# The opening of a hybrid decoder step: normalization in a written order, first weights by pairs of contraction tiles

## The chip, the core and the metric

The program runs on one core of a Trainium2 chip. A core has TensorE (PE, matmuls; PEld loads its stationary operand), VectorE (DVE), ScalarE (ACT), GpSimd (POOL) and SyncE (SP), each with an in-order queue of its own, and 16 DMA engines that move data between the chip's main memory and the on-chip memory SBUF. Matmuls write to PSUM, which has 8 banks of 128 x 512 fp32 here. The metric is the device time of one execution in microseconds (us); a change is judged by the medians of several executions.

## What is computed

One layer of a decoder with two branches, for 512 prompt rows behind 16 learned meta rows and for 8 x 4 sample rows with paged keys and values of the past (560 rows in all, model width 2048, 8 heads of 128):

```python
h = rmsnorm(x, g_pre)
q, k, v, ga, cb, cc, ch, gc, ma, mc = jnp.split(h @ w_in, split_offsets(), axis=-1)
a = attend(q, k, v, b_sb).reshape(bsz, t, D_ATTN) * jax.nn.silu(ga)      # stick-breaking attention
u = cc * ch
u_ext = jnp.concatenate([conv_hist, u], axis=1)
c = cb * causal_conv(u_ext, w_conv, b_conv) * jax.nn.silu(gc)
merged = sigmoid(ma + b_gate[:D_MODEL]) * (a @ w_pa) + sigmoid(mc + b_gate[D_MODEL:]) * (c @ w_pc)
y = x + rmsnorm(merged @ w_out, g_post)

def rmsnorm(x, g):
    y = x * lax.rsqrt(jnp.mean(x * x, axis=-1, keepdims=True) + RMS_EPS)
    return y * g
```

Products are wanted at fp32 accuracy. The kernel splits each operand into a high part in the format fp32r (a rounded copy, made by ACT) and a low part (the rest, made by DVE), and makes three products of them: high x high, low row part x high weight part, high row part x low weight part.

## The kernel before

The kernel is written in a layer that builds in-order queues for the engines from one program. A scheduler decides the order within each queue by a timing model of its own, except for instructions that are pinned (`pin`, which is `tc.keep_in_program_order`): these stay in the order in which the source gives them. `tc.high_priority` moves an instruction forward in the scheduler's choice.

The change lies in the opening stage, from the start to the end of the first four heads' query products ("the first weights", `FIRST = 4`):

- The 560 rows come as five tiles `xt` (tiles 0 to 3 of 128 rows, tile 4 of 48). For each, ACT squares and sums a row (`sq`, `ss`), takes a first inverse root by Ln and Exp (`rstd_of`), and five small operations refine it (`newton`, giving `rs`). DVE multiplies one half of the columns with `rs` and the broadcast gains `g_bc` (`hn`, 128x1024). PE transposes `hn` in 128x128 blocks into PSUM tiles of four blocks, ACT rounds each tile to `h_hi`, and DVE subtracts to get `h_lo`. Half 0 of a tile gives contraction tiles k = 0 to 7, half 1 gives k = 8 to 15.
- PSUM tiles of the transposes rotate over `z`, `z`, `z`, `tp` (`start_ps`). A tile is free again when DVE has made `h_lo` of it.
- The first weights come as eight raw tiles of 512 KB, two to a head (1024 rows of the weight by 128 columns each), with 512 bytes in a run. ACT makes `whi` of each. All four heads are first multiplied over 256 rows (tiles 0 and 1) with the high weight part alone, `q_part(..., (0, 1), ...)`. The low weight parts `wlo` are made later, from `low()`, after the other row tiles' normalization. Then each head gets its third product and the remaining 296 rows. The result of the 256 rows is copied to `qf` and stored.
- The queue SP issues the loads in the order x0, x1, two weight tiles, x4, six weight tiles, x2, x3.

After that the pool of the opening stage (`start`, called `sp` in the code) is closed, and what follows uses its room: `bsb` (head biases), `pt_i` (the page table of the sample rows' cache), `bg`, `wcv`, `stc`, and the tiles of the heads. The key, value and query products of the heads follow (`proj`, `gemm`, each of two 1024-row weight units with three split buffers, `whl`). Beside them run the steps of the sample rows' attention (`dec_step`): POOL reads page numbers out of `pt_i` into registers (32 of them), loads key pages `kpage` and queries `qb` (the latter from `q_scr`, to which POOL has stored the transposed queries `qn`), and DVE multiplies them (`pr`). `natural` transposes keys and values back into `nat`, one buffer, which POOL stores to the outputs.

Of the kernel before, what the change touches and what calls it, by code (L numbers as in the profile page):

```python
# [9 lines left out]
F32 = mybir.dt.float32  # L10
# [7 lines left out]
P = 128  # L18
D = 2048
# [41 lines left out]
def hybrid_step_kernel(  # L61
# [64 lines left out]
    def rstd_of(eng, out, ss, tmp, n, w=1, later=False):  # L126

        v, r, t = (tmp[:n, i * w:(i + 1) * w] for i in range(3))
        act.activation(r, ss, AF.Ln, bias=eps_c[:n], scale=1.0 / D)
        act.activation(r, r, AF.Exp, scale=-0.5)  # L130

        def newton(pin=lambda ins: ins):
            pin(eng.tensor_scalar(out=v, in0=ss, scalar1=1.0 / D, scalar2=EPS, op0=ALU.mult, op1=ALU.add))
# [3 lines left out]
            pin(eng.tensor_mul(out, r, t))  # L137
# [40 lines left out]
        g_ps.append(pt)  # L178

    def g_copy(c):  # L180
        pin(dve.tensor_copy(g_bc[:, c * 512:(c + 1) * 512], g_ps[c]))

    start_ps = cycle((z_ps, z_ps, z_ps, t_ps))

    def norm_stats(i):

        n = sum(r[0] for r in XT[i][0])
        xt = sp.tile([P, D], F32, name="xt", bufs=3)[:n]
        load_x(xt, i)
        ss = sp.tile([P, 1], F32, name="ss", bufs=5)[:n]  # L190
        sq = sp.tile([P, D], F32, name="sq", bufs=1)[:n]
        rs = sp.tile([P, 1], F32, name="rs", bufs=5)[:n]
        tmp = sp.tile([P, 4], F32, name="rtmp", bufs=5)
        with tc.high_priority():
            act.activation(sq, xt, AF.Square, accum_out=ss)
            newton = rstd_of(dve, rs, ss, tmp, n, later=True)
        return (i, n, xt, rs), newton

    def norm_half(c, x):


        i, n, xt, rs = x
        hn = sp.tile([P, D // 2], F32, name="hn", bufs=4)[:n]
        cs = slice(c * 1024, (c + 1) * 1024)
        pin(dve.scalar_tensor_tensor(out=hn, in0=xt[:, cs], scalar=rs, in1=g_bc[:n, cs],
                                     op0=ALU.mult, op1=ALU.mult))
        low = []
        for kq in range(2):
            pt = next(start_ps)()
            pv = pt[:, :4 * n].rearrange("p (k t) -> p k t", t=n)  # L210
            with tc.high_priority(2000):
                for k in range(4):
                    pe.transpose(out=pv[:, k, :], in_=hn[:, (4 * kq + k) * P:(4 * kq + k + 1) * P],
                                 identity=ident[:n, :n])
            k0 = 8 * c + 4 * kq
            for r0, r1, t0 in XT[i][1]:
                dst = (slice(None), slice(k0, k0 + 4), slice(t0, t0 + r1 - r0))
                with tc.high_priority(2000):
                    act.copy(h_hi[dst], pv[:, :, r0:r1])
                low.append((h_lo[dst], pv[:, :, r0:r1], h_hi.bitcast(F32)[dst]))  # L220

        def lows():
            for x in low:
                pin(dve.tensor_sub(*x))
        return lows


    def w_load(src, pl=wraw):
        raw = pl.tile([P, 8, P], F32, tag="raw", name="raw", bufs=5 if pl is wraw else 2 * FIRST - 5)
# [31 lines left out]
    def win_srcs(c):  # L261
        return [win[0:1024, c:c + P], win[1024:2048, c:c + P]]
# [20 lines left out]
    w_low = []

    def low(n=1):

        for _ in range(n):
            unit, raw = w_low.pop(0)
            lo = whl.tile([P, 8, P], F32R, tag="lo", name="wlo")
            pin(dve.tensor_sub(lo, raw, unit[0].bitcast(F32)))  # L290
            unit.append(lo)

    def q_part(o, ws, n, parts, start, stop):
        t0, t1 = START[n]
        for k in range(KD):
            for m in parts:
                pe.matmul(o, lhsT=ws[k // 8][m // 2][:, k % 8, :], rhs=(h_lo if m == 1 else h_hi)[:, k, t0:t1], start=(start and k + m == 0),
                          stop=(stop and k == KD - 1 and m == parts[-1]), skip_group_check=True)

    q_w, q_o = [], []  # L300

    def q_load(h):
        q_w.append([])
        for src in win_srcs(GATE_Q + h * P):
            n = len(w_low)
            raw = w_load(src, sp if n >= 5 else wraw)
            hi = sp.tile([P, 8, P], F32R, name="whi", bufs=2 * FIRST - 3) if n >= 3 else \
                whl.tile([P, 8, P], F32R, tag="hi", name="whi")
            act.copy(hi, raw)
            q_w[h].append([hi])  # L310
            w_low.append((q_w[h][-1], raw))

    x0, newton0 = norm_stats(0)
    x1, newton1 = norm_stats(1)
# [30 lines left out]
    l21 = norm_half(1, x2)
    l20()
    newton3(pin)
    l30 = norm_half(0, x3)
    l21()
    l31 = norm_half(1, x3)  # L350
    l30()
    low()
    l31()
    low()
    for h in range(FIRST):
        q_part(q_o[h], q_w[h], 0, (2,), False, True)
        qf = sp.tile([P, 256], F32, name="qf", bufs=2)
        act.activation(qf, q_o[h], AF.Copy, scale=SCALE)
        pool.dma_start(qt_scr[h][:, 0:256], qf)
        q_o[h] = (z_ps if h < 3 else mm_ps)()[:, :START[1][1] - START[1][0]]  # L360
        q_part(q_o[h], q_w[h], 1, (0, 1, 2), True, True)
        low(min(len(w_low), 2))
    stx.close()


# [956 lines left out]
```

## Time and profile before

| | |
|---|---|
| three runs, us | 1642.79, 1644.03, 1644.74 (median 1644.03) |
| profiled execution, us | 1641.85; its span from first to last instruction 1640.3 |
| mean granted TensorE clock of that execution | 0.99 |
| PE busy | 1594.9 us of the span, 97% |
| DVE, ACT, POOL busy | 1251.8, 970.1, 232.4 us |
| PE busy in 0 to 27, 27 to 54, 54 to 86.5 us | 15.08, 24.27, 32.50 us |
| last first-weights product starts | 86.27 us |

Busy times are what an engine worked, not what it had to; a PE that is busy need not be at its peak, since matmuls overlap. A row of the timeline gives the start, the length, the engine, the source line, the operation, out<-in with shape and count, and in brackets the idle time of that engine just before with the instruction that ended it. The stage tables give the busy time of each engine in a stretch, with PEclk, the clock that the throttle granted (1.00 is full).

### The profile page before, as it was taken

The page shows a single profiled execution, that of the slowest core. Times are in us where ns is not written, and L with a number is a line of the kernel's source. Part 1 is how long each engine was busy: PE and PEld are TensorE (multiplying, and loading weights), DVE is VectorE, ACT ScalarE, POOL GpSimd, SP SyncE. Part 2 cuts the span into 40 slices and gives each one's busy share as a digit, 9 for nine tenths or more (in the row PEclk, how much of TensorE's full clock was granted, in tenths as well). Part 3 has the DMA queues.
Part 4 walks back from the last instruction along what each step waited for, and adds up shares of the span by engine and source line. Part 5 has one row for each costly group of instructions (what it writes and reads, how often), then busy time and mean ns, then how long its engine had stood idle before and what let it go on. Part 6 is the DMA issues. An engine that isn't in the chain of part 4 may idle for free.

```text
span 1640.3 us, 31584 instructions
## 1 busy us (share of the span) xinstructions
PE 1594.9 (97%) x12176; PEld 1531.3 (93%) x12176; DVE 1251.8 (76%) x1707; ACT 970.1 (59%) x2529; POOL 232.4 (14%) x414
## 2 busy tenths in 40 slices
PE   7999999999999999999999999999999999999996
PEld 6999999999999999999999999989867699999995
DVE  4537887797988988888988888876555567877774
ACT  5237887745765655655677667685544543455552
POOL 0033233322101010101011010013122110000000
PEclk7999999999999999999999999999999999999998
DMA  9255454445544444443455454446887555433336
GB/s 228 70 179 152 155 160 139 146 128 170 157 147 136 136 135 122 127 142 111 137 164 161 149 174 148 135 125 204 283 261 222 172 152 179 154 106 94 104 87 216
DMA packets 306492, 252.72 MB, mean 154 GB/s; under 512 B 11457, under 2 KB 276741, under 8 KB 305237
## 3 DMA queue, kind: packets, MB, share of 16 engines
q1 hardware_dynamic: 277605, 159.73, 34.1%
q0 software_dynamic: 28016, 88.80, 16.5%
q8 instruction: 95, 1.56, 0.4%
q10 hardware_dynamic: 720, 2.17, 0.4%
q14 instruction: 56, 0.46, 0.1%
HBM read 217.95 MB, written 32.71 MB: 153 GB/s over the span
## 4 chain that ended last, share of the span: by engine, by line
PE 75%; ACT 6%; DMA 5%; DVE 5%; issue 3%; POOL 0%; DVEq 0%; SPq 0%; POOLq 0%; ACTq 0%
PE mm L887 24%; PE mm L252 24%; PE o L887 19%; ACT junk L695 3%; PE tp L784 2%; ACT whi L236 2%; DMA raw<-in_w_in 2%; PE z L614 1%; PE o L624 1%; DVE pr L689 1%; DVE wlo L237 1%; DMA gt<-gate_scr 1%; PE z L545 1%; PE z L887 1%; DMA kpage<-in_cache_k 1%
## 5 line engine op out<-in xcount | busy, mean ns | idle before, releaser
L236 ACT CAST whi<-raw 128x1024 fp32r<-128x1024 f32 x251 | 263.1, 1050 | 258.5 <-PE o L887 79.3
L237 DVE TENSOR_TENSOR wlo<-raw,whi 128x1024 fp32r<-128x1024 f32 x251 | 306.4, 1221 | 58.0 <-ACT whi L236 46.1
L887 PE MATMUL mm<-h_hi,whi 128*128 128x272 f32 (+1 forms) x1152 | 333.5, 290 | 2.8 <-ACT whi L236 2.8
L887 PE MATMUL mm<-h_lo,whi 128*128 128x272 f32 (+1 forms) x1152 | 332.1, 288 | 0.0
L887 PE MATMUL mm<-h_hi,wlo 128*128 128x272 f32 (+1 forms) x1152 | 331.3, 290 | 0.0
L887 PE MATMUL o<-t_hi,whi 128*128 128x272 f32 (+1 forms) x864 | 252.2, 292 | 8.5 <-ACT o L901 5.9
L887 PE MATMUL o<-t_hi,wlo 128*128 128x272 f32 (+1 forms) x864 | 249.9, 289 | 1.4 <-DVE wlo L237 1.4
L887 PE MATMUL o<-t_lo,whi 128*128 128x272 f32 (+1 forms) x864 | 249.6, 289 | 0.0
L237 DVE TENSOR_TENSOR wlo<-s,whi 128x1024 fp32r<-128x1024 f32 x126 | 154.2, 1224 | 101.5 <-ACT whi L236 101.2
L887 PEld LDWEIGHTS mm<-h_hi,whi 128*128 128x128 f32 x1152 | 217.3, 189 | 5.5 <-ACT whi L236 3.7
L887 PEld LDWEIGHTS mm<-h_hi,wlo 128*128 128x128 f32 x1152 | 216.3, 189 | 0.6 <-DVE dr L412 0.4
L887 PEld LDWEIGHTS mm<-h_lo,whi 128*128 128x128 f32 x1152 | 216.8, 188 | 0.1
L695 ACT ACTIVATE junk<-pr 128x128 f32<-128x128 f32 x592 | 182.7, 309 | 28.3 <-DVE pr L689 16.1
L236 ACT CAST whi<-s 128x1024 fp32r<-128x1024 f32 x126 | 131.6, 1044 | 97.5 <-PE o L887 31.0
L252 PE MATMUL mm<-h_hi,whi 128*128 128x280 f32 (+1 forms) x640 | 187.1, 293 | 0.0
L252 PE MATMUL mm<-h_hi,wlo 128*128 128x280 f32 (+1 forms) x640 | 187.0, 293 | 0.0
L252 PE MATMUL mm<-h_lo,whi 128*128 128x280 f32 (+1 forms) x640 | 186.7, 292 | 0.0
L887 PEld LDWEIGHTS o<-t_hi,whi 128*128 128x128 f32 x864 | 162.7, 188 | 15.1 <-ACT o L901 7.0
L887 PEld LDWEIGHTS o<-t_hi,wlo 128*128 128x128 f32 x864 | 162.9, 189 | 2.3 <-DVE wlo L237 2.2
L887 PEld LDWEIGHTS o<-t_lo,whi 128*128 128x128 f32 x864 | 163.4, 189 | 0.0
L689 DVE TENSOR_TENSOR pr<-kpage,qb 128x1024 f32<-128x1024 f32 x128 | 152.3, 1218 | 8.4 <-DMA kpage<-in_cache_k 4.0
L252 PEld LDWEIGHTS mm<-h_hi,whi 128*128 128x128 f32 x640 | 120.5, 188 | 0.7
(389 smaller groups left out, 3398.2 us busy)
## 6 DMA issues: line engine op xcount, KB each, us to landing
raw<-in_w_in SPq DMA_DIRECT2D x192, 512.0 KB, 4.3
kpage<-in_cache_k POOLq DMA_DIRECT2D x64, 256.0 KB, 3.4
qb<-q_scr POOLq DMA_DIRECT2D x32, 512.0 KB, 5.3
vpage<-in_cache_v POOLq DMA_DIRECT2D x64, 256.0 KB, 5.7
raw<-in_w_out SPq DMA_DIRECT2D x32, 512.0 KB, 4.0
gate_scr<-g POOLq DMA_DIRECT2D x32, 272.0 KB, 3.2
gt<-gate_scr POOLq DMA_DIRECT2D x16, 544.0 KB, 4.2
raw<-in_w_pc SPq DMA_DIRECT2D x16, 512.0 KB, 5.8
```

Of the source, the lines that this page charges most:

```text
L236: act.copy(hi, x)
L237: dve.tensor_sub(lo, x, hi.bitcast(F32))
L252: pe.matmul(o, lhsT=w, rhs=r[:, t0:t1], start=(k == 0 and n == 0), stop=(k == nk - 1 and n == 2))
L545: pe.matmul(zt[:m, c0:c0 + n], lhsT=l[:, s0:s0 + m], rhs=r[:, ts:ts + n], start=(c0 == 0 and i == 0), stop=(i == 2), skip_group_check=True)
L614: pe.matmul(o, lhsT=l, rhs=x, start=False, stop=(i == len(ops) - 1), skip_group_check=True)
L624: pe.matmul(ot[:, ts - NMETA:ts - NMETA + n], lhsT=l[:m, st, :], rhs=x[:m, c0:c0 + n], start=False, stop=(g == GROUPS[-1] and i == 2), ski ...
L689: dve.tensor_mul(pr, kt.unsqueeze(1).broadcast_to([P, 2, 512]), qt))
L695: act.activation(junk, pr[:, t, h * P:(h + 1) * P], AF.Copy, accum_out=z_all[:, pg, b, 4 * hf + h, 2 * i + t:2 * i + t + 1])
L784: pe.matmul(po[32 * j:32 * (j + 1), :], lhsT=lhs, rhs=rhs, start=(pg == 0), stop=(pg == NPG), tile_position=(0, 32 * j), skip_group_check= ...
L887: pe.matmul(o, lhsT=l[:, k, :], rhs=r, start=(start and k == 0 and m == 0), stop=(stop and k == 7 and m == 2), skip_group_check=True)
```

## The change

- **Order.** All steps of the opening stage on PE, ACT, DVE and SP are pinned: `pin` stands on the loads of x, the squares, Ln and Exp, the transposes, the `h_hi` copies, and the products. The source gives one order for all.
- **Gains.** Of the four copies that make `g_bc`, DVE keeps two and ACT makes two.
- **First weights by contraction tiles.** `q_load` now loads two contraction tiles k (256 weight rows) for all four heads at once: 512 KB in runs of 2 KB. `q_chunk(c)` makes, for k = 2c and 2c + 1, all three products of each head over the 256 rows. Both weight parts of all eight raw tiles stay in SBUF until the remaining 296 rows are multiplied.
- **PSUM.** Two heads share one bank (two tiles `mm` instead of three `mm` and one `o`); the freed `o` joins the rotation of the transposes.
- **Row tiles.** Tiles 0 and 1 come first, then chunks 0 to 7 of the products with tile 2 (between chunks 2 and 4) and tile 4 (before chunk 5) between them, and tile 3 after chunk 7. The refinement `newton` of tiles 2 and 4 is made on POOL.
- **Room.** The opening pool holds five `whi` and five `wlo` instead of five `whi` and three raw tiles. Tiles opened later, `bsb` and `pt_i` among them, now lie in its room.

```diff
     def load_x(xt, i):
...
-            nc.sync.dma_start(xt[r:r + n, :], {"p": xp, "m": meta_tokens, "s": xs}[src][r0:r0 + n, :])
+            tc.keep_in_program_order(
+                nc.sync.dma_start(xt[r:r + n, :], {"p": xp, "m": meta_tokens, "s": xs}[src][r0:r0 + n, :]))
...
     def g_copy(c):
-        pin(dve.tensor_copy(g_bc[:, c * 512:(c + 1) * 512], g_ps[c]))
-
-    start_ps = cycle((z_ps, z_ps, z_ps, t_ps))
+        copy = dve.tensor_copy if c < 2 else act.copy
+        pin(copy(g_bc[:, c * 512:(c + 1) * 512], g_ps[c]))
+
+    start_ps = cycle((z_ps, z_ps, z_ps, t_ps, o_ps))
...
-        with tc.high_priority():
-            act.activation(sq, xt, AF.Square, accum_out=ss)
-            newton = rstd_of(dve, rs, ss, tmp, n, later=True)
-        return (i, n, xt, rs), newton
+        pin(act.activation(sq, xt, AF.Square, accum_out=ss))
+        return (i, n, xt, rs), rstd_of(eng, rs, ss, tmp, n, later=True, fix=pin)
...
+    def q_load():
+        c = len(q_raw)
+        raw = wraw.tile([P, 8, P], F32, tag="raw", name="raw")
+        pin(nc.sync.dma_start(raw.rearrange("p (k h) c -> p k (h c)", k=2),
+                              win[2 * c * P:2 * (c + 1) * P, GATE_Q:GATE_Q + FIRST * P].rearrange(
+                                  "(k p) c -> p k c", p=P)))
+        q_raw.append(raw)
+
+    def q_part_tile(c, name):
+        if c < 3:
+            return whl.tile([P, 8, P], F32R, tag=name, name="w" + name)
+        return sp.tile([P, 8, P], F32R, name="w" + name, bufs=NC - 3)
...
+    def q_product(o, h, k, n, start, stop):
         t0, t1 = START[n]
...
+        hi, lo = (by_k(x[k // 2])[:, k % 2, h, :] for x in (q_hi, q_lo))
+        for m, (l, r) in enumerate(((hi, h_hi), (hi, h_lo), (lo, h_hi))):
+            pin(pe.matmul(o, lhsT=l, rhs=r[:, k, t0:t1], start=(start and m == 0), stop=(stop and m == 2),
+                          skip_group_check=True))
...
+    def q_chunk(c):
+
+        for h in range(FIRST):
+            for k in (2 * c, 2 * c + 1):
+                q_product(q_o[h], h, k, 0, k == 0 and h % 2 == 0, k == KD - 1)
...
+    newton1(pin)
+    q_high()
+    h10, l10 = norm_half(0, X[1])
+    h01()
     l00()
+    h11, l11 = norm_half(1, X[1])
+    h10()
+    X[4] = x_load(4)
...
+    l10()
+    q_high()
+    q_low()
+    h11()
+    q_chunk(0)
     l01()
+    q_low()
     l11()
...
+    q_chunk(7)
+    newton3(pin)
...
     for h in range(FIRST):
...
         q_o[h] = (z_ps if h < 3 else mm_ps)()[:, :START[1][1] - START[1][0]]
-        q_part(q_o[h], q_w[h], 1, (0, 1, 2), True, True)
-        low(min(len(w_low), 2))
+        for k in range(KD):
+            q_product(q_o[h], h, k, 1, k == 0, k == KD - 1)
     stx.close()
```

What the change makes of the queues is shown at three places. Line numbers of the changed kernel differ from those of the profile: L213 becomes L216, L297 becomes L321, L224 becomes L228, L205 becomes L209, L290 becomes L315, L373 and L374 become L436 and L437, L666 becomes L729.

PE, from the broadcast of the gains (L175) to the first products, before (the alternating rows of a tile's second half on `tp` are left out after the first two):

```order
L175 MATMUL z<-g_hl,pick 128x128 x8
L213 MATMUL z<-ident,hn 128x128 x9
L213 MATMUL tp<-ident,hn 128x128
...
L213 MATMUL z<-ident,hn 128x128 x8
L297 MATMUL mm<-h_hi,whi 128x256 x3
L213 MATMUL z<-ident,hn 128x128
L213 MATMUL tp<-ident,hn 128x128
...
L297 MATMUL mm<-h_lo,whi 128x256
L297 MATMUL mm<-h_hi,whi 128x256
```

The same place of PE in the changed kernel:

```order
L176 MATMUL z<-g_hl,pick 128x128 x8
L216 MATMUL z<-ident,hn 128x128 x12
L216 MATMUL tp<-ident,hn 128x128 x4
L216 MATMUL o<-ident,hn 128x128 x4
L216 MATMUL z<-ident,hn 128x128 x12
L321 MATMUL mm<-h_hi,whi 128x256
L321 MATMUL mm<-h_lo,whi 128x256
L321 MATMUL mm<-h_hi,wlo 128x256
```

All 32 transposes of tiles 0 and 1 now stand ahead of the first product, and each product with the low weight part stands beside the other two.

DVE, from the second refinement (its last row is L137) on, before:

```order
L137 TENSOR_TENSOR rs<-rtmp 128x1
L205 SCALAR_TENSOR_TENSOR hn<-xt,rs,g_bc 128x1024
L224 TENSOR_TENSOR h_lo<-z,h_hi 128x4x128 x3
L224 TENSOR_TENSOR h_lo<-tp,h_hi 128x4x128
L205 SCALAR_TENSOR_TENSOR hn<-xt,rs,g_bc 128x1024
L224 TENSOR_TENSOR h_lo<-z,h_hi 128x4x128 x3
L224 TENSOR_TENSOR h_lo<-tp,h_hi 128x4x128
```

DVE at the same place of the changed kernel:

```order
L138 TENSOR_TENSOR rs<-rtmp 128x1
L209 SCALAR_TENSOR_TENSOR hn<-xt,rs,g_bc 128x1024
L228 TENSOR_TENSOR h_lo<-z,h_hi 128x4x128 x2
L209 SCALAR_TENSOR_TENSOR hn<-xt,rs,g_bc 128x1024
L228 TENSOR_TENSOR h_lo<-o,h_hi 128x4x128
L228 TENSOR_TENSOR h_lo<-z,h_hi 128x4x128
L315 TENSOR_TENSOR wlo<-raw,whi 128x1024
L228 TENSOR_TENSOR h_lo<-z,h_hi 128x4x128
L228 TENSOR_TENSOR h_lo<-tp,h_hi 128x4x128
L315 TENSOR_TENSOR wlo<-raw,whi 128x1024
```

The second `hn` of tile 1 moved ahead of two of tile 0's four subtractions, and the low weight parts moved in among them.

POOL, from the identity matrix on (the 32 readings of `pt_i` follow each other before; `st_n` is the conv state, `bg_n` and `wc_n` are the gate biases and conv weights), before:

```order
masks.py:197 MEMSET ident 128x128
L373 DMA bsb<-in_b_sb 128x8
L374 DMA pt_i<-in_page_table 1x16x2
...
L149 AFFINE_SELECT tri<-tri 128x128
L666 TENSOR_LOAD pt_i
L666 ISA x2
...
L359 DMA qt_scr<-qf 128x256 x4
L377 DMA bg_n<-in_b_gate 32x128
```

POOL of the changed kernel, from the end of the refinement of tile 4 on (the rows that read `pt_i` go on, 32 in all, between the stores of the queries, `q_scr`):

```order
L138 TENSOR_TENSOR rs<-rtmp 48x1
L421 DMA qt_scr<-qf 128x256 x4
L436 DMA bsb<-in_b_sb 128x8
L437 DMA pt_i<-in_page_table 1x16x2
L440 DMA bg_n<-in_b_gate 32x128
...
L445 DMA st_n<-in_state_conv 16x1024
L535 DMA qt_scr<-qr 128x288 x2
L729 TENSOR_LOAD pt_i
L729 ISA x2
...
L541 DMA q_scr<-qn 32x128
```

The loads of `bsb` and `pt_i` moved from the start of the program to behind the stores of the first weights' results, where they wait for the last product of that stage, and the 32 readings moved with them.

More of the change, by code (lines that the diff above doesn't have):

```diff
@@ L122, in load_x, with rstd_of @@
         for n, src, r0 in XT[i][0]:
[L123 removed]
+            tc.keep_in_program_order(
+                nc.sync.dma_start(xt[r:r + n, :], {"p": xp, "m": meta_tokens, "s": xs}[src][r0:r0 + n, :]))
             r += n
[L126 removed]
+    def rstd_of(eng, out, ss, tmp, n, w=1, later=False, fix=lambda ins: ins):
         v, r, t = (tmp[:n, i * w:(i + 1) * w] for i in range(3))
[L129 to L130 removed]
+        fix(act.activation(r, ss, AF.Ln, bias=eps_c[:n], scale=1.0 / D))
+        fix(act.activation(r, r, AF.Exp, scale=-0.5))
         def newton(pin=lambda ins: ins):
@@ L189, in norm_stats @@
         load_x(xt, i)
+        return i, n, xt
+    def norm_stats(x, eng=dve):
+        i, n, xt = x
         ss = sp.tile([P, 1], F32, name="ss", bufs=5)[:n]
@@ L206, in norm_half @@
                                      op0=ALU.mult, op1=ALU.mult))
-        low = []
+        parts = []
         for kq in range(2):
@@ L210, in norm_half, with highs, w_load @@
             pv = pt[:, :4 * n].rearrange("p (k t) -> p k t", t=n)
[L211 to L214, printed above, removed]
+            for k in range(4):
+                pin(pe.transpose(out=pv[:, k, :], in_=hn[:, (4 * kq + k) * P:(4 * kq + k + 1) * P],
+                                 identity=ident[:n, :n]))
             k0 = 8 * c + 4 * kq
             for r0, r1, t0 in XT[i][1]:
[L217 to L220, printed above, removed]
+                parts.append(((slice(None), slice(k0, k0 + 4), slice(t0, t0 + r1 - r0)), pv[:, :, r0:r1]))
+        def highs():
+            for dst, src in parts:
+                pin(act.copy(h_hi[dst], src))
         def lows():
[L223 to L229, printed above, removed]
+            for dst, src in parts:
+                pin(dve.tensor_sub(h_lo[dst], src, h_hi.bitcast(F32)[dst]))
+        return highs, lows
+    def w_load(src):
+        raw = wraw.tile([P, 8, P], F32, tag="raw", name="raw")
         nc.sync.dma_start(raw, src.rearrange("(k p) c -> p k c", p=P))
@@ L282, in hybrid_step_kernel @@
     START = ((HM, HM + 256), (HM + 256, T))
[L283 to L293, printed above, removed]
-        t0, t1 = START[n]
[L295 to L314, printed above, removed]
@@ L318, in hybrid_step_kernel, with keep_warm @@
+    q_o = []
+    def q_chunk(c):
+        for h in range(FIRST):
+            for k in (2 * c, 2 * c + 1):
+                q_product(q_o[h], h, k, 0, k == 0 and h % 2 == 0, k == KD - 1)
+    def keep_warm(n):
+        pass
+    X = [None] * 5
+    X[0], X[1] = x_load(0), x_load(1)
+    for _ in range(3):
+        q_load()
+    X[2] = x_load(2)
+    X[0], newton0 = norm_stats(X[0])
     g_copy(0), g_copy(1)
+    g_copy(2), g_copy(3)
+    X[1], newton1 = norm_stats(X[1])
     newton0(pin)
-    l00 = norm_half(0, x0)
@@ L321, in hybrid_step_kernel @@
-    g_copy(2), g_copy(3)
-    l01 = norm_half(1, x0)
+    h00, l00 = norm_half(0, X[0])
+    keep_warm(4)
+    h01, l01 = norm_half(1, X[0])
+    keep_warm(6)
+    h00()
     newton1(pin)
-    l10 = norm_half(0, x1)
+    q_high()
+    h10, l10 = norm_half(0, X[1])
+    h01()
     l00()
+    h11, l11 = norm_half(1, X[1])
+    h10()
+    X[4] = x_load(4)
+    for _ in range(2):
+        q_load()
+    for i in range(2):
+        o = mm_ps()
+        q_o += [o[:, 0:256], o[:, 256:512]]
+    l10()
+    q_high()
@@ L345, in hybrid_step_kernel @@
[L345 to L356, printed above, removed]
+    q_high()
+    q_chunk(1)
+    X[2], newton2 = norm_stats(X[2], pool)
+    q_low()
+    for _ in range(2):
+        q_load()
+    q_chunk(2)
+    X[4], newton4 = norm_stats(X[4], pool)
+    newton2()
+    h20, l20 = norm_half(0, X[2])
+    q_high()
@@ new lines, in hybrid_step_kernel @@
+    q_low()
+    q_load()
+    X[3] = x_load(3)
+    h20()
+    q_chunk(3)
+    h21, l21 = norm_half(1, X[2])
+    q_high()
+    l20()
+    q_low()
+    h21()
+    newton4()
+    q_chunk(4)
+    h40, l40 = norm_half(0, X[4])
+    l21()
+    q_high()
+    h40()
+    q_low()
+    h41, l41 = norm_half(1, X[4])
+    q_chunk(5)
+    l40()
+    h41()
+    q_high()
+    q_low()
+    l41()
+    q_chunk(6)
+    q_high()
+    q_low()
+    X[3], newton3 = norm_stats(X[3])
+    q_chunk(7)
+    newton3(pin)
```

41 lines of the change are left out of this document (21 added, 20 removed).

## The prediction

> **What bounds the kernel now.** The page's first part says PE; so a gain has to be PE time that is idle or slow. The table by stage (columns: stretch and its length, PE, PEld, DVE, ACT and POOL busy, granted clock, share of the DMA engines, GB/s) shows where that is.
>
> ```profile
> PE 1594.9 (97%) x12176; PEld 1531.3 (93%) x12176; DVE 1251.8 (76%) x1707; ACT 970.1 (59%) x2529; POOL 232.4 (14%) x414
> 0.00:10.00 10.00, 8.62 (x42) 7.05 (x42) 4.00 (x17) 3.78 (x5) 2.15 (x9) 0.96 0.80 231
> 10.00:20.00 10.00, 3.88 (x16) 3.13 (x16) 5.13 (x10) 5.46 (x7) 0.00 (x0) 0.50 1.17 216
> 20.00:30.00 10.00, 5.58 (x26) 5.18 (x27) 5.06 (x7) 8.71 (x15) 0.00 (x0) 0.51 1.09 281
> 25.00:30.00 5.00, 3.62 (x18) 3.62 (x19) 2.93 (x4) 3.71 (x5) 0.00 (x0) 0.53 1.02 250
> 30.00:40.00 10.00, 10.00 (x89) 9.62 (x88) 5.46 (x10) 5.28 (x8) 0.00 (x0) 1.00 0.84 206
> 40.00:50.00 10.00, 7.52 (x65) 7.35 (x64) 7.71 (x24) 4.92 (x16) 0.00 (x0) 1.00 0.01 3
> 54.00:86.50 32.50, 32.50 (x247) 32.50 (x247) 12.43 (x12) 5.16 (x8) 2.21 (x4) 1.00 0.35 103
> 86.50:120.00 33.50, 33.50 (x264) 32.61 (x263) 10.93 (x16) 14.76 (x46) 11.98 (x22) 1.00 0.56 172
> ```
>
> From 10 to 30 us PE works 9.5 of 20 us, at half clock; 2.5 more are idle before 50; from 54 on it is full at full clock. The gain can only come from the first 54 us, and a loss can start anywhere that this full stretch is broken. PE's timeline says what it waits for in the weak part.
>
> ```profile
> 22.07 1.97 PE L213 MATMUL z<-ident,hn 128*128 128x128 f32 x8 [6.80 <-DVE h_lo L224]
> 26.39 1.01 PE L297 MATMUL mm<-h_hi,whi 128*128 128x256 f32 x3 [2.35 <-ACT h_hi L219]
> 29.33 0.41 PE L297 MATMUL mm<-h_lo,whi 128*128 128x256 f32 x1
> 29.54 0.36 PE L297 MATMUL mm<-h_hi,whi 128*128 128x256 f32 x1
> 30.09 0.28 PE L297 MATMUL mm<-h_hi,whi 128*128 128x256 f32 x1
> 30.21 0.28 PE L297 MATMUL mm<-h_lo,whi 128*128 128x256 f32 x1
> 44.93 1.06 PE L213 MATMUL z<-ident,hn 128*128 128x128 f32 x8 [2.48 <-DVE hn L205]
> 86.13 0.30 PE L297 MATMUL mm<-h_lo,whi 128*128 128x296 f32 x1
> 86.40 0.29 PE L252 MATMUL mm<-h_hi,whi 128*128 128x280 f32 x1
> ```
>
> It waits for the normalization chain (6.80 for an `h_lo`, 2.35 for an `h_hi`), not for weights. The first product starts at 26.39 and the opening ends at 86.40, where the first key product starts. The pitch of products is 0.21 in the slow clock (29.33 to 29.54) and 0.12 in the full one (30.09 to 30.21); with 296 columns it is 0.135 (86.13 to 86.40, two products); a transpose at full clock takes 0.11 ((1.06 - 0.27) / 7).
>
> **The front chain in the written order.** These rows of ACT and DVE give the durations.
>
> ```profile
> 10.28 1.91 ACT L195 ACTIVATE sq<-xt 128x2048 f32<-128x2048 f32 x1 [1.71 <-DMA xt<-in_x_prompt]
> 12.10 0.19 ACT L195 ACTIVATION_READ_ACCUMULATOR sq<-xt 128x1 f32 x1
> 12.19 1.03 ACT L309 CAST whi<-raw 128x1024 fp32r<-128x1024 f32 x1
> 13.12 0.29 ACT L129 ACTIVATE rtmp<-ss,eps_c 128x1 f32<-128x1 f32 x1
> 15.49 1.04 ACT L309 CAST whi<-raw 128x1024 fp32r<-128x1024 f32 x1 [2.08 <-DMA raw<-in_w_in]
> 16.44 0.20 ACT L130 ACTIVATE rtmp<-rtmp 128x1 f32<-128x1 f32 x1
> 22.82 0.57 ACT L219 CAST h_hi<-z 128x512 fp32r<-128x512 f32 x1
> 8.54 0.14 DVE L133 TENSOR_SCALAR rtmp<-ss 128x1 f32<-128x1 f32 x1
> 9.19 0.16 DVE L137 TENSOR_TENSOR rs<-rtmp 128x1 f32<-128x1 f32 x1
> 9.38 1.28 DVE L205 SCALAR_TENSOR_TENSOR hn<-xt,rs,g_bc 128x1024 f32<-128x1024 f32 x1
> 10.58 0.68 DVE L181 COPY g_bc<-mm 128x512 f32<-128x512 f32 x1
> 26.65 1.28 DVE L224 TENSOR_TENSOR h_lo<-z,h_hi 128x512 fp32r<-128x512 f32 x2
> L290 DVE TENSOR_TENSOR wlo<-raw,whi x8: 1209/1222/1227, 34.9 to 74.9; 128x1024 fp32r<-128x1024 f32 x8
> ```
>
> Before, the Exp of tile 1 stood behind two weight casts, the second of which waited for its raw tile, so it ran at 16.44 although its squares were done at 12.3. The written order puts nothing between. ACT gets two gain copies (about 0.57 each, the nearest row is the 128x512 `h_hi`), which push the squares of tile 1 from 10.28 to 10.6. Squares 1.91 + 0.19, Ln 0.29, Exp 0.20 end at 13.2; the five small operations, 0.81 from 8.54 to 9.35 in the rows, end `rs` at 14.1. DVE then, with starts 0.08 closer than the durations (9.38 to 10.58): `hn` 1.2, two `h_lo` 1.2, `hn` 1.2, two `h_lo` 1.2, one `wlo` 1.14, and one more `h_lo` 0.6, which frees the `z` that the last four transposes of tile 1 need: 20.7. Transposes at slow clock 0.84 and a hand-over of 0.15: **first product at 21.7 instead of 26.39.** The two copies DVE loses cost nothing there, since it waits for `rs` anyway.
>
> **From the first product to the end of the stage.** The count of products is the same: 192 of 256 rows x 0.12 = 23.0, 192 of 296 x 0.135 = 25.9, 48 transposes of tiles 2, 3, 4 x 0.11 = 5.3. The slow clock adds: in the rows PE's unbroken work began at 26.39 and the pitch changed at 29.7, 3.3 us later. If it takes 3.3 us again, 16 products cost 0.09 more each, 1.4; if the rise stays at 29.7 for another reason, 38 products, 3.4. I take 2.0, nearer to the first, since 26.39 is the only such start here. Waits in between I put at 0.6: one, for `hn` of tile 4's second half, as DVE makes the rest (`h_lo`, `wlo`) ahead of PE; the 296-row products start right behind tile 3, whose `h_lo` end within its transposes. Sum: 21.7 + 23.0 + 25.9 + 5.3 + 2.0 + 0.6 = **78.5 against 86.40, a gain of 7.9** (7.0 to 8.5 by the two ends of the clock and no wait).
>
> On the clock the Trainium skill has a rule, in "TensorE: Matmul & The Clock Gate", section "Part 1: The HAM clock gate": it rises after one fully busy window of about 3.4 us, and windows run free. The 3.3 us agree with it; by that rule the rise would fall between 25.1 and 28.5 here, and the stage would end between 77.9 and 79.4.
>
> Two heads in a bank, and both weight parts kept, cost room and no time: each `wlo` is made once, as before (8 x 1.22), earlier. The loads are hidden: the tables above give 2.3 MB by 10 us, 4.5 by 20, 7.3 by 30, and the order needs x0, x1 and three weight tiles (3.5 MB) by about 22 and x2, x4 and a fourth (5.4 MB) by 28.5. On SP, x4 waits for tile 0's buffer (its second `hn`, 12.0), and the fourth and fifth weight tiles behind it are needed 16 us later; the last three wait for buffers freed from about 20 on, and are needed from 37.
>
> **What lies behind the stage.** `bsb` and `pt_i` now wait on POOL for the stage's last product, and the 32 readings of `pt_i` move from hidden time to POOL's busiest stretch, ahead of the stores of the sample queries.
>
> ```profile
> L666 POOLq TENSOR_LOAD <-pt_i x32: 282/289/502, 9.6 to 28.3; - x32
> DMA to landing us min/median/max: 7.4/7.4/7.4
> bg_n<-in_b_gate POOLq DMA_DIRECT2D x1, 16.0 KB, 2.0
> 87.02 0.51 POOL L377 DMA_DIRECT2D bg_n<-in_b_gate  x1 [5.69 <-PE mm L297]
> 109.12 0.50 POOL L478 DMA_DIRECT2D q_scr<-qn  x1 [3.10 <-ACT qn L477]
> 117.48 5.70 DMA out<-nat
> 123.92 0.28 PE L445 MATMUL tp<-ident,raw 128*16 128x128 f32 x1 [1.13 <-ACT nat L443]
> ```
>
> A reading takes (28.3 - 9.6) / 31 = 0.60, all of them 19.3. `bg_n` was issued 0.6 behind the stage's end; two issues go ahead of it, and eight issues at about 0.53 put the first reading at +4.8 of the end, unless `pt_i` takes as long to land as at the start (7.4, then +8.5; the row of `bg_n`, issued in the same place, says 2.0). The fourth `q_scr` is issued at +24.1 if the DMA issues between the readings run beside them, +28.4 if after them (8 x 0.54), +32.1 if `pt_i` is late too; before it was +22.7 (109.12 - 86.40). So POOL's chain (query store, `qb`, then `out<-nat`, which frees `nat`) lags by 1.4 to 9.4; I take 4, near the case with `pt_i` quick. PE already waited 1.13 for `nat` at the value head's transposes, and these stand 27 products (3.4 us) later in PE's new order. So the wait becomes 1.13 + 4 - 3.4 = 1.7, **0.6 more than before** (bounds: 1.1 less, 6.0 more). From there on queues hold the same work.
>
> Total: 1641.85 (span 1640.3 and 1.55 around it) - 7.9 + 0.6 = 1634.5 for an execution like the profiled one. That one is 2.2 below the median, so against the median **1636.7**.
>
> **Refinement on POOL.** No row shows these small operations there. The nearest are POOL's selects of small tiles:
>
> ```profile
> L562 POOL TENSOR_SCALAR_AFFINE_SELECT r<-r x16: 190/308/3417, 144.0 to 292.1; 128x128 f32<-128x128 f32 x12, 16x16 f32<-16x16 f32 x4
> L562 POOL TENSOR_SCALAR_AFFINE_SELECT eA<-eA x4: 278/282/282, 161.9 to 303.7; 128x112 f32<-128x112 f32 x4
> ```
>
> Five at 0.28 are 1.4, five at the longest 17. Tile 2's Exp ends at about 26.0 by the durations above, and PE needs its first transposes only behind chunk 2 at 32.1, so up to some 4.8 us are covered. Beyond, DVE stands at `hn` with the `wlo` of later chunks queued behind it, and tile 4 comes behind tile 2 on POOL, so each us costs two. I take 1.5, by the medians.
>
> **Rivals.** (1) *The readings hold the queries.* At the far end, 9.4 of lag, PE loses 6.0 of the 7.9: 1644.03 - 7.9 + 6.0 = about 1642. For it: every issue on POOL stands in one queue, and nothing shows a reading beside an issue. Against: it needs the late `pt_i` as well. (2) *The other side: the refinement on POOL stretches.* At a length p the loss is 2 x (p - 4.8): the gain of 7.3 is gone at p = 8.5, the kernel is measurably slower above p = 10.1, and at p = 17 it takes about 1661. For it: the 3417 ns row, and DVE at work all the while beside it. Against: the medians. The Trainium skill, "SBUF — State Buffer", section "SBUF: two separate sides", calls the port pair of DVE and GpSimd an exclusive lock; whether the 3417 ns row is that, no run here shows. A form of this rival with a size of its own: if each of the five waits out one DVE instruction of 1.28, p is 5 x 1.56 = 7.8, and the time 1636.7 + 6.0 = 1642.7; that is what the lock of that page would make. (3) *A cast holds ACT.* In a strict order all of ACT stands behind a weight cast whose raw tile is late, as at 15.49 (2.08 of idle time). If the first raw tile comes one tile's transfer late (512 KB at 216 GB/s, 2.4 us) and the next one by 0.5, the first product starts at 24.6 and the time is about 1639.6. Against: x0, x1 and the first weight tiles lead the queue as before, and the first cast comes only at 14.1, where it ran at 12.19 without a wait.
>
> **How the numbers follow.** The forecast's case gets 60%: 1633 to 1639, from the ends of the clock, the waits and the smaller lags. Rival 1 gets 18%, rival 3 12%, rival 2 10%, half of it at 1642.7 and half slower than before. The range is 1633.0 to 1643.5: it takes in rivals 1 and 3 and leaves out the slow half of rival 2 and some of each end. 0.2% is 3.3 us, about what this kernel's runs can tell from no change. Faster by more (below 1640.7): nearly all of the forecast's case, most of rival 3 and a quarter of rival 1, 0.74. Within: most of rival 1, the mild rival 2, 0.18. Slower: 0.08.
>
> **What the new profile would show.** The first product at 21 to 22.5, PE full from there with a granted clock of 1.00 from about 26, no wait over 1 us, and the first key product at 78 to 80. The five operations of tile 2 on POOL within 2 us from about 26. On POOL, readings from about 5 us behind the stage's end, the last query store 24 to 32 behind it, and at the value head's transposes a PE wait of 0 to 4. I am wrong if PE waits for `hn` of tile 2 (rival 2), if ACT stands at a weight cast before 20 (rival 3), or if PE waits 5 us or more for `nat` (rival 1).

## The result: slower, though the opening stage is 10.6 us shorter

The changed kernel takes 1648.41 us in the median (1644.81 to 1651.14) against 1644.0; the ratio is 1.0029, with a 95% interval of 1.0021 to 1.0037. The execution that was profiled (1650.27) lies 1.9 above its median and that of the kernel before 2.2 below its own, so the two traces differ by 8.2 where the medians differ by 4.4.

The table by stage of the changed kernel, same columns as before:

```profile
10.00:20.00 10.00, 7.92 (x34) 6.78 (x35) 8.80 (x15) 8.64 (x15) 0.00 (x0) 0.50 1.05 216
20.00:30.00 10.00, 10.00 (x77) 10.00 (x77) 8.23 (x9) 7.20 (x11) 5.64 (x10) 0.87 1.00 307
100.00:110.00 10.00, 8.18 (x67) 7.91 (x65) 3.14 (x3) 3.97 (x8) 1.83 (x4) 1.00 0.41 117
110.00:120.00 10.00, 6.00 (x42) 5.79 (x41) 3.57 (x5) 2.58 (x13) 4.45 (x7) 0.91 0.77 246
390.00:400.00 10.00, 7.67 (x61) 7.45 (x60) 0.96 (x2) 3.78 (x4) 0.29 (x1) 1.00 0.93 283
400.00:410.00 10.00, 6.20 (x33) 6.20 (x34) 10.00 (x13) 4.84 (x19) 1.30 (x3) 0.66 0.29 85
```

The opening did what it was meant to: PE is full from 20 us on, but for 0.76 us at 38. What is new are two holes further back, at 100 to 120 us and at 390 to 410. Before, PE was full from 86.5 to 120, and between 390 and 410 it idled 2.2 us, in one wait (the last row is of the list of PE's waits: engine, output and line that waited, what it waited for; us, times, longest):

```profile
400.00:410.00 10.00, 7.76 (x62) 7.54 (x61) 6.04 (x7) 4.33 (x13) 1.58 (x3) 1.00 0.89 303
PE o L887 <- ACT o L901: 2.2, 1, 2.2
```

In PE's timeline of the changed kernel:

```profile
17.68 2.22 PE L216 MATMUL z<-ident,hn 128*128 128x128 f32 x8 [0.51 <-DVE hn L209]
19.55 0.56 PE L321 MATMUL mm<-h_hi,whi 128*128 128x256 f32 x1
22.77 0.28 PE L321 MATMUL mm<-h_hi,whi 128*128 128x256 f32 x1
22.89 0.28 PE L321 MATMUL mm<-h_lo,whi 128*128 128x256 f32 x1
38.45 0.42 PE L216 MATMUL o<-ident,hn 48*128 48x48 f32 x4 [0.76 <-DVE hn L209]
75.79 0.29 PE L256 MATMUL mm<-h_hi,whi 128*128 128x280 f32 x1
```

The first product starts at 19.55 (before 26.39), and the first key product at 75.79 (before 86.40). The two holes, in the list of PE's waits:

```profile
PE tp L505 <- DVE ks L511: 4.0, 1, 4.0
PE tp L538 <- ACT qn L540: 2.3, 2, 1.8
PE o L950 <- DVE c L976: 6.1, 1, 6.1
```

Both kernels issue the same matmuls, so the lead can be followed: take the start of PE's n-th matmul and subtract its start in the profile of the kernel before (a minus is earlier). Matmul 600 lies at 99 us of the kernel before, 1000 at 152, 2600 at 361, 3200 at 439, 12100 at 1615, near the end. The kernels below are those of the experiments, with one execution for each, so a row also holds what differs from execution to execution.

| kernel | 600 | 1000 | 2600 | 3200 | 12100 |
|---|---|---|---|---|---|
| changed | -10.6 | -4.0 | -3.9 | 5.3 | 8.2 |
| changed, second execution | -11.8 | -8.4 | -7.3 | 0.8 | 1.0 |
| pages early | -9.6 | -9.1 | -8.9 | -1.2 | 1.6 |
| copies first | -8.3 | -3.7 | -3.7 | 5.9 | 8.2 |
| query loads later | -11.8 | -7.8 | -6.7 | -2.5 | -0.3 |
| pages early and query loads later | -9.5 | -6.1 | -5.9 | -1.4 | -0.6 |
| pages and copies first, which gives the order of before at the switch | -11.1 | -9.7 | -9.7 | -8.3 | -9.6 |
| before, pages late | -0.7 | 3.7 | 3.8 | 5.2 | 8.8 |
| before, both loads late, which gives the order of the changed kernel at the switch | -3.3 | -0.7 | -0.7 | 7.5 | 10.1 |

**The first loss, 6.6 us between matmuls 600 and 1000 (3.4 in the second execution).** Rows of POOL, and one of ACT:

```profile
L729 POOLq TENSOR_LOAD <-pt_i x32: 283/288/499, 82.4 to 106.1; - x32
102.35 0.26 ACT L540 COPY qn<-tp 32x128 f32<-32x128 f32 x1 [4.15 <-DMA q_scr<-qn]
107.21 0.50 POOL L541 DMA_DIRECT2D q_scr<-qn  x1 [3.50 <-ACT raw L581]
110.39 2.18 POOL L744 DMA_DIRECT2D qb<-q_scr  x3 [2.68 <-issue]
```

The query loads of the kernel before:

```profile
111.41 2.18 POOL L681 DMA_DIRECT2D qb<-q_scr  x3 [1.78 <-issue]
```

The chain of waits of the changed kernel in that stretch:

```profile
110.39 5.54 DMA qb<-q_scr
116.03 1.23 DVE pr L752
117.25 0.19 DVE nat L510
117.44 0.21 DVE ks L511
```

The 32 readings run from 82.4 to 106.1, with the query stores among them. PE is held in two places. The first is `qn`, which has one buffer: ACT copies into it only when the store before has landed, and with the stores late ACT waits (4.15 in its row) and PE's transposes wait 2.3 us for ACT. In the kernel before POOL waited for `qn` (3.10 ahead of its store at 109.12) and not the other way round. The second is behind the queries. The query loads are issued 34.6 us behind the opening's end (110.39 - 75.79), where the kernel before needed 25.0 (111.41 - 86.40): a lag of 9.6. `pr` waits for the queries, DVE's two copies out of the key head's transposes stand behind `pr`, and the next transposes need the PSUM tile that these copies free (4.0 us). Behind that the granted clock falls (0.91 from 110 to 120).

**The second loss, 9.2 us between matmuls 2600 and 3200 (8.1 in the second execution).** This is where the gate products follow the heads; below it is called the switch. The rows are: of the chain of waits, the weight tile; of POOL, the loads of the sample rows' second part; of the answer on the tile `raw` between 387 and 390, the two issues and how long the tiles took to land (min/median/max).

```profile
387.84 11.93 DMA raw<-in_w_in
386.47 1.47 POOL L744 DMA_DIRECT2D qb<-q_scr  x2 [2.88 <-issue]
387.93 1.66 POOL L730 DMA_DIRECT2D kpage<-in_cache_k  x3
389.57 0.71 POOL L744 DMA_DIRECT2D qb<-q_scr  x1
L234 SPq DMA_DIRECT2D raw<-in_w_in x2: 367/368/368, 387.8 to 388.9; - x2
DMA to landing us min/median/max: 11.9/12.3/12.7
```

The same of the kernel before:

```profile
394.47 1.49 POOL L681 DMA_DIRECT2D qb<-q_scr  x2 [4.67 <-DMA raw<-in_w_in]
L230 SPq DMA_DIRECT2D raw<-in_w_in x2: 368/368/368, 388.7 to 389.8; - x2
DMA to landing us min/median/max: 4.1/4.1/4.1
```

In the changed kernel POOL's burst of 2.25 MB (three `qb` of 512 KB, three `kpage` of 256 KB) is issued from 1.4 us ahead of two weight tiles, which land after 12 us instead of 4. DVE idles (0.96 busy from 390 to 400), PE waits 6.1 us for `c`, and its clock falls (0.66 from 400 to 410). Before, the burst stood behind the landing of these tiles; a later tile, issued at 395.3 within it, took 9.8 us to land.

The burst is not all of this loss. Followed matmul by matmul, 3.0 us go between matmuls 2760 and 2800, around 380 us and so ahead of the burst, where PE waits 0.7, 0.6 and 0.7 in turn for `nat`, a weight cast and a `wlo`; 8.5 go between 2880 and 2920, at the wait for `c` and in the slow clock behind it; and 2.6 come back at the place where the kernel before has its own wait of 2.2.

### The profile page after: what moved, and what is told of

The parts are those of the page before. It is cut to its first block, busy times and chain, and to the rows that moved or that the text cites. A ratio compares the mean times of both kernels' runs of the same rounds, so it can differ in the third digit from the quotient of the medians.

```text
span 1648.7 us, 31575 instructions
## 1 busy us (share of the span) xinstructions
PE 1600.4 (97%) x12176; PEld 1536.7 (93%) x12176; DVE 1246.8 (76%) x1695; ACT 970.9 (59%) x2531; POOL 236.4 (14%) x424
## 4 chain that ended last, share of the span: by engine, by line
PE 74%; ACT 6%; DMA 6%; DVE 4%; issue 3%; DVEq 0%; POOL 0%; SPq 0%; ACTq 0%; POOLq 0%
PE mm L950 24%; PE mm L256 24%; PE o L950 19%; ACT junk L758 3%; DMA raw<-in_w_in 3%; PE tp L847 2%; ACT whi L240 2%; PE z L677 1%; PE o L687 1%; DVE pr L752 1%; DVE wlo L241 1%; DMA gt<-gate_scr 1%; PE z L608 1%; PE z L950 1%; DMA cr<-c_scr 0%
```

## The experiments

**A second execution of the changed kernel.**

> The changed kernel as it is, a second profiled execution. It looks 10.6 us ahead of the kernel before when the opening stage ends (75.79 against 86.40), 3.5 to 4 ahead from 125 to 380 us, and 5 behind from 415 us on. If both losses are built into its order, they stand again at the same places: about 7 us at the first head's value transposes (105 to 120 us), and 5 to 9 us around 385 to 405 us. If the second is an accident of one execution, it is under 2 us here. Time about 1648.

Measured: 1646.69, ratio 1.0024 (1.0012 to 1.0037). The time is 1.3 under the expected one, and both losses stand again, the first at half its size:

```profile
PE tp L505 <- DVE ks L511: 2.7, 1, 2.7
PE o L950 <- DVE c L976: 4.6, 1, 4.6
```

They belong to the kernel, and the size of the first changes from execution to execution.

**The readings: taken out of the changed kernel, and put into the kernel before.**

```diff
+    bsb, pt_i = const.tile([P, H], F32, name="bsb"), const.tile([1, DB * NPG], I32, name="pt_i")
+    pool.dma_start(bsb, ...), pool.dma_start(pt_i, ...)        # ahead of the opening
...
-    bsb = dp.tile([P, H], F32, name="bsb")
-    pt_i = dp.tile([1, DB * NPG], I32, name="pt_i")
-    pool.dma_start(bsb, b_sb.broadcast_to([P, H]))
-    pool.dma_start(pt_i, page_table.rearrange("b p -> (b p)").unsqueeze(0))
```

> bsb and pt_i in the pool of constants, loaded at the start, so that the 32 readings run at 9 to 30 us as in the kernel before. Theory A (the readings delay the stores of the sample queries, so the query loads, so DVE's pr, behind which stand the copies that free the transposes' PSUM tile): the last query store at about 76 + 23 = 99 instead of 107, no PE wait over 1.5 us between 85 and 125, and about 7 us less: 1641 to 1642 where the second loss stays, 1635 to 1638 where it goes as well. Rival (the loss at 105 to 120 comes from the places that the value transposes got in PE's order, or from late weight tiles): still over 4 us of PE waits there, 1646 to 1650.

Measured: 1643.62, ratio 1.0001 (0.9992 to 1.0010), so 0.23% (3.8 us) better than the changed kernel in its second execution. The last query store went from 107.21 to 100.01, the first loss from 6.6 or 3.4 to 0.5, and the waits for `qn` and `ks` are gone. Theory A says so for `ks`; `qn` it had not named. The second loss stayed whole (7.7). In PE's waits and at the two weight tiles:

```profile
PE tp L508 <- ACT nat L506: 1.8, 1, 1.8
PE o L950 <- DVE c L976: 4.2, 1, 4.2
L234 SPq DMA_DIRECT2D raw<-in_w_in x2: 367/368/368, 382.8 to 383.9; - x2
DMA to landing us min/median/max: 11.3/12.1/12.9
```

The other way round, in the kernel before:

```diff
-    pool.dma_start(pt_i, page_table.rearrange("b p -> (b p)").unsqueeze(0))
+    act.copy(pt_i.bitcast(F32), q_o[FIRST - 1][0:1, 0:DB * NPG]); pool.dma_start(pt_i, ...)
```

> The kernel before with one thing of the change: pt_i is loaded only after the last product of the opening stage (a copy of a row of that product's PSUM tile into pt_i ahead of the load makes it wait), so that the 32 readings stand between the query stores. PE, DVE and SP keep their order up to there. Theory A: the last query store moves from 109 to 116 to 119, the first qb lands 7 to 9 us later, PE waits 4 to 7 us at the transposes of the first heads, and the time is 1648 to 1652. Rival (the readings are hidden, the loss of the changed kernel comes from its own order): within 2 us of the kernel before, 1642 to 1646.

Measured: 1644.99, ratio 1.0007 (0.9999 to 1.0016), a time in the rival's range. The edit makes less than the change does: 21 of the 32 readings stand ahead of the last query store (from 92.1 on; in the changed kernel all 32), and the rest run on to 123. The last query store moved by 1.6 only, since POOL had been idle 2 to 3 us ahead of each of the last three stores in the kernel before, and the readings filled that. The query loads moved from 111.41 to 115.04, PE waits 2.9 in a place where it had not, and 4.4 us are lost between matmuls 600 and 1000 in this execution; the ratio shows about 1.2, and its interval does not exclude none. So in the kernel before a loss by the readings is not shown by the times. In the changed kernel it is: 3.8 us by the ratios, 3.4 to 6.6 in the traces, and the smaller of the two losses.

**By which path the readings reach PE.** The low part of the keys is pinned behind DVE's copies out of the transposes, and the copies then stand ahead of the first `pr`:

```diff
-        split_evac(khi, klo, kr, kr)
+        act.copy(khi, kr), pin(dve.tensor_sub(klo, kr, khi.bitcast(F32)))
```

> The changed kernel with the readings where they are, but with DVE's two copies out of the first key head's transposes pinned ahead of the first pr (through the low part of the keys, which is pinned behind them), so that the PSUM tile tp is free without the queries. If PE's wait at the first value head comes through DVE (tp is freed only behind pr, which waits for qb), that wait of 2.7 to 4 us goes and the kernel is 2 to 4 us faster than the changed one's 1646.7: 1643 to 1645. If POOL's lag holds PE through nat as the prediction had it (the store of nat to the outputs stands behind qb on POOL), the wait only moves on, to the second transposes of the value head, with 3 us or more there, and the time stays at 1645.5 to 1648.

Measured: 1645.78, ratio 1.0016 (1.0005 to 1.0027), which its interval does not part from the changed kernel's 1.0024 (1.0012 to 1.0037). The wait for `ks` went, two waits for `qn` (1.0 and 0.9) stayed, and one for `nat` appeared:

```profile
PE tp L508 <- ACT nat L506: 2.2, 1, 2.2
```

Between matmuls 600 and 1000 4.6 us are lost, within the 3.4 to 6.6 without the edit. So DVE's `pr` is not the only path; `qn` is another, which neither the prediction nor the theories of these runs saw. The path through `nat`, the only one of the prediction, is not shown to come from the readings: with the pages early PE waits as long for it (1.8 above, 2.9 and 2.6 in two kernels below).

**The second loss: the query loads moved behind the weight tiles** (shortened; the key pages' loads of these units are pinned too).

```diff
+                        # first query load of the second part alone; its first two units' loads are pinned
+                        pin(pool.memset(qt, 0.0)), pin(pool.memset(qt, 0.0))
-                        pool.dma_start(qt, q_scr[r0:r0 + 2, cs]...)
+                        pin(pool.dma_start(qt, q_scr[r0:r0 + 2, cs]...))
```

> The changed kernel with two memsets ahead of the first query load of the second part of the sample rows' steps, and that part's first loads pinned, so that the query loads (1.5 MB) leave 386 to 392 us and only the three key pages (0.75 MB) stay. Theory B (the loads of POOL's burst share the DMA engines with two weight tiles issued at 387.8 and 388.9, which take 11.9 us instead of 4, and DVE and PE wait for them): these weight tiles land in under 7 us, PE loses under 3 us between 375 and 415 us against the kernel before instead of 9, and the time is 1641 to 1645. Rival (the wait there is made by DVE's own order of rows): PE still loses 7 to 9 us there and the time stays at 1647 to 1650. The first loss of 7 stays in both.

Measured: 1642.04, ratio 0.9997 (0.9986 to 1.0008), 0.27% (4.4 us) better than the changed kernel in its second execution. `qb` is issued at 402.43; the weight tiles share the DMA engines with the three key pages alone:

```profile
L234 SPq DMA_DIRECT2D raw<-in_w_in x2: 368/368/368, 385.1 to 386.2; - x2
DMA to landing us min/median/max: 5.8/6.1/6.4
```

The wait for `c` is gone, so theory B holds for it, though the pins also gave PE another order from matmul 2892 on. Of the 8.1 us of the second execution 4.2 remain at matmul 3200: 4.3 are lost in the first products of the switch, where PE waits in turn for `nat`, a cast and a `wlo` and the clock falls (0.66 from 380 to 385), 2.5 come back, and 2.4 are lost between matmuls 3060 and 3140, with a wait of 1.4 for a cast. The 4.3 can't come from the burst, whose first load is issued behind these waits, at 383.79.

**Both edits.**

> bsb and pt_i at the start and the query loads of the second part behind the weight tiles, both edits together. If the two losses are separate (the readings at 90 to 120 us, the shared DMA engines at 388 to 400 us), the gains add: the changed kernel measured 1646.7, the first edit gave 3.1, the second 4.7, so 1638 to 1640, faster than both kernels, with PE 8 to 9 us ahead of the kernel before up to 370 us and 4 to 5 ahead at 445. Rival (whatever is gained ahead of 370 us is lost again at the switch from heads to gate products, because DVE or the weight stream sets the pace there): 1642 or more, and PE less than 2 us ahead at 445.

Measured: 1637.48, ratio 0.9971 (0.9961 to 0.9981), faster than both kernels. The gains add, by the ratios to the kernel before (0.53% under the changed kernel; 0.23 and 0.27 alone), though the lead at 439 us is 1.4, not 4 to 5: in the profiled execution, the slowest of the twelve (1641.26), PE lost 3.4 in the first place as well, with a wait of 2.9 for `nat`, and 4.5 at the switch. The first loss is thus 0.5 to 3.4 in the four traces with the changed opening and the pages early (1.4 and 2.1 in the two that follow below), and 3.4 to 6.6 in the four with the pages late (4.0 and 4.6 behind the two of the changed kernel).

**The clock.** The kernel with both edits, and three matmuls of constants in PE's two gaps among tile 1's transposes.

> The kernel with both edits, with two 128x512 matmuls of constants in PE's gap ahead of the first transposes of tile 1's first half and one in the gap ahead of its second half, so that PE has no idle time from 10.7 us on. If the clock rises behind a stretch without idle time, as in the kernel before (3.3 us behind 26.39) and the changed one (22.5, 4.8 us behind its last gap), it now rises by 17.5 us, all products of 256 rows run at 0.12, and the opening ends 1.3 to 2.2 us earlier than without them: 1637 to 1638. Rival (the rise at 22.5 has another reason, or the three matmuls hold the transposes): the clock rises at 22 to 23 as before, the opening ends 0 to 0.8 later.

Measured: 1637.77, ratio 0.9974 (0.9963 to 0.9985). The time is the expected one, but says nothing: the clock did rise early, but so it did without the three matmuls. The row of the same transposes in the changed kernel, and in the one with both edits:

```profile
15.19 1.12 PE L216 MATMUL o<-ident,hn 128*128 128x128 f32 x4 [0.82 <-DVE hn L209]
15.23 0.66 PE L216 MATMUL o<-ident,hn 128*128 128x128 f32 x4 [0.91 <-DVE hn L209]
```

**Whether the second loss is the order of rows, or the price of coming early.** All kernels with the changed opening so far, however far ahead they come (3.7 to 8.9), lose 4 to 10 us at the switch; the kernel before with `pt_i` late loses 1.4. But all of the former have also another order there. On PE, `before` has 26 gate products, four transposes of the last value head, 22 products, and the last two transposes; the changed kernel has 24 products, all six transposes, 24 products. On DVE, two `wlo` that stand among the sums before the switch have another place, and the copies out of the last transposes stand earlier. Nobody wrote either order: the scheduler works it out from its model of the whole program. Two kernels part the explanations. The first takes the changed opening, `bsb` and `pt_i` early, and the pin on the low part of the keys; with these the scheduler gives PE, DVE, ACT and POOL the order of before at the switch, without a difference on PE from matmul 2703 to 9069. The early loads alone and the pin alone do not: in both of these kernels PE keeps the 24, six and 24. The second has the opening of before and makes both loads late, which brings the changed kernel's order there, on PE up to matmul 2891:

```diff
-    pool.dma_start(bsb, b_sb.broadcast_to([P, H]))
-    pool.dma_start(pt_i, page_table.rearrange("b p -> (b p)").unsqueeze(0))
+    act.copy(bsb, q_o[FIRST - 1][:, 0:H]); pool.dma_start(bsb, ...)
+    act.copy(pt_i.bitcast(F32), q_o[FIRST - 1][0:1, 0:DB * NPG]); pool.dma_start(pt_i, ...)
```

> The kernel with bsb and pt_i at the start, and with the low part of the keys pinned behind DVE's copies out of the transposes. The pin makes the scheduler give PE, DVE, ACT and POOL the same order of rows at the switch from the heads to the gate products as in the kernel before (26 gate products ahead of the last value head's transposes, query loads behind the weight tiles), with the changed kernel's opening. Theory B in its wider form (the loss of 7.7 to 9 us between 370 and 415 us belongs to the order of rows there): PE keeps its lead through the switch, 7 us or more ahead of the kernel before at 440 us against 1.2 with the pages early alone, and the time is 7 us or more under the kernel before, 1633 to 1637. Rival (whoever comes earlier to the switch loses the lead there, since DVE or the weight tiles set the pace): the lead shrinks to under 3 us, 1640 to 1643.

> The kernel before, opening untouched, but bsb and pt_i loaded only after the last product of the opening stage, both by a copy out of that product's PSUM tile. With both late the scheduler gives the order of rows of the changed kernel at the switch to the gate products (24 gate products, then all of the last value head's transposes; query loads right behind its stores), with no gain ahead of it. Theory B in its wider form: 7 to 9 us are lost between 370 and 415 us, on top of 1 to 4 from the readings, 1650 to 1655. Rival (the loss there comes from arriving early): no loss there, 1643 to 1646 as with the pages late alone.

Measured: the first 1634.41, ratio 0.9951 (0.9935 to 0.9967); the second 1651.71, ratio 1.0045 (1.0028 to 1.0061). The first keeps 8.3 of its 9.7 us through the switch, the second loses 8.2 there without any gain ahead. The query loads and the weight tiles of the first:

```profile
384.67 1.49 POOL L744 DMA_DIRECT2D qb<-q_scr  x2 [4.66 <-DMA raw<-in_w_in]
L234 SPq DMA_DIRECT2D raw<-in_w_in x2: 367/368/368, 379.1 to 380.2; - x2
DMA to landing us min/median/max: 3.9/4.4/4.9
```

and of the second:

```profile
390.06 1.46 POOL L681 DMA_DIRECT2D qb<-q_scr  x2 [3.25 <-issue]
L230 SPq DMA_DIRECT2D raw<-in_w_in x2: 368/368/368, 391.1 to 392.2; - x2
DMA to landing us min/median/max: 10.3/10.3/10.3
PE o L887 <- DVE c L913: 4.8, 1, 4.8
```

The second loss is the order, not the lead: it goes where a kernel that leads by 9.7 has the order of before, and comes where one with no lead has the other. What turned the order is less clear. In the kernel before, it stayed with `pt_i` alone late and turned with both loads late; in the changed kernel both loads early did not turn it back, and it took the pin as well. So the late loads are enough to turn it, and in the changed kernel they are not all that does.

## Why the prediction was wrong, step by step

- **The front chain was right in kind, and its sum 2.1 too long.** The first product came at 19.55, not 21.7. The last transposes did not wait for the `wlo` and the `h_lo` that the sum put ahead of them; eight transposes started right behind `hn` at 17.68, the last four of them at 18.78, when the `h_lo` ahead of that `wlo` had ended (18.73) and freed a buffer. That takes 1.7 off the sum.
- **The rest of the opening was right.** Pitch 0.12, one wait for `hn` of tile 4's second half (0.76 against 0.6), and 3.2 us of slow clock behind the first product. It ended at 75.79, not 78.5. Over the eight profiles with this opening it ends at 74.6 to 78.1, over the three with the opening of before at 83.1 to 86.4; the means differ by 8.9, so 10.6 is a large case and the forecast 7.9 a little small. Its bounds of 7.0 to 8.5 are too narrow by its own terms: the late rise of the clock with the wait gives 6.5, the early one without it 9.1.
- **The refinement on POOL (rival 2) was not it.** It took 2.2 us for tile 2 and 4.2 for tile 4, under the 4.8 that were covered, although four of the ten operations did wait out a DVE instruction, as that rival had it; PE waited for neither.
- **No cast held ACT (rival 3).** ACT's first cast ran at 13.90 without a wait.
- **The lag behind the stage was mis-sized.** The prediction took 4 out of 1.4 to 9.4, at the last query store; there the trace has 8.7 (107.21 - 75.79 against 22.7), and 9.6 at the query loads, the far end of rival 1. The page table came neither quick nor late (it landed after 4.7, between the 2.0 and the 7.4 of the sum), and the readings and the issues between them ran one after the other, 23.7 us for the 32. The term "0.6 more than before" measured 6.6 and 3.4 in two executions. Its path was wrong too: in the changed kernel PE did not wait for `nat` there, but for `qn` and for the copies behind DVE's `pr`. That its sum with 9.6 in place of 4 gives 6.2 more, near the 6.6, is luck.
- **The step that failed is "From there on queues hold the same work".** The work is the same, its order is not, and that order cost 8 to 9 us 300 us later. The 0.6 that became 3.4 to 6.6 and this together turn a gain of 10.6 into a loss. In the range of 1633.0 to 1643.5 no case had a price behind the first heads, though PE's order differs from that of before as far as matmul 3085. The rival on the other side was put on POOL's small operations, where it was not.

With the loads of `bsb` and `pt_i` early and the pin on the low part of the keys, which bring back the order of before at the switch, the kernel takes 1634.4, 2.3 under the forecast 1636.7: the opening is worth at least what the forecast gave it. That is an argument for the sum of the opening, not for the forecast, which was for another kernel.

## What to carry to other kernels

Where a scheduler orders the queues, an edit in one stage is also an edit of every later stage whose rows it reorders: compare the whole order, and price each place where a burst of loads passes the tiles that the bound engine's chain waits for. Look at what a new claim on room pushes back: here two loads of 4 and 0.1 KB, which had cost nothing at the start, brought 32 register readings into a busy queue, and made late in the kernel before they turned the order by themselves. Follow the lead of the bound engine's n-th instruction through two traces; the places where it shrinks are where to look for the causes, and a stage that gained what was wanted is no proof of a gain.

## What the hardware showed that was not expected

**Small operations on POOL wait out DVE's.** Rows of POOL, and of DVE beside it (tile 4's refinement has five operations, of which four stand here):

```profile
25.91 1.14 POOL L134 TENSOR_SCALAR rtmp<-ss 48x1 f32<-48x1 f32 x1 [0.23 <-ACT sq L200]
27.13 0.19 POOL L135 TENSOR_TENSOR rtmp<-rtmp 48x1 f32<-48x1 f32 x1
27.40 1.24 POOL L136 TENSOR_TENSOR rtmp<-rtmp 48x1 f32<-48x1 f32 x1
28.72 1.10 POOL L137 TENSOR_SCALAR rtmp<-rtmp 48x1 f32<-48x1 f32 x1
25.72 1.29 DVE L209 SCALAR_TENSOR_TENSOR hn<-xt,rs,g_bc 128x1024 f32<-128x1024 f32 x1 [1.20 <-POOL rs L138]
27.36 1.23 DVE L315 TENSOR_TENSOR wlo<-raw,whi 128x1024 fp32r<-128x1024 f32 x1 [0.36 <-ACT whi L310]
28.50 1.28 DVE L209 SCALAR_TENSOR_TENSOR hn<-xt,rs,g_bc 128x1024 f32<-128x1024 f32 x1
```

One takes 0.19 while DVE is idle (27.13), and 1.10 to 1.24 when it starts inside a DVE instruction, to whose end it lasts. The Trainium skill, "SBUF — State Buffer", section "SBUF: two separate sides", calls the port pair of DVE and GpSimd an exclusive lock; these rows agree with it. Of the ten small operations four met one.

**The clock does not rise at a fixed time behind the first work.** With the same opening it was up at 15.2 us in one execution and at 22.5 in another, as the two rows on the clock and the pitch of products show; in the second execution of the changed kernel itself it was up at 15.2 too (the same four transposes in 0.67). The Trainium skill, "TensorE: Matmul & The Clock Gate", section "Part 1: The HAM clock gate", says that the window it watches, of about 3.4 us, runs free, which makes the point of the rise vary. The spread here is 7.3, more than one such window, so the gaps of 0.5 to 1.2 us among the transposes may count as well; no run here parts the two or fixes the window's phase.
